# Encoder block: softmax scaling ahead of the fillers, gates by tanh, half of branch B's maxima on VectorE, first remainders on VectorE

## Chip, core and metric

The kernel runs on one core of a Trainium2 chip. The metric is the device time of one execution in microseconds (us). TensorE is called PE below, VectorE DVE, ScalarE ACT, GpSimd POOL and SyncE, which issues the DMAs, SP.

## The reference

One encoder layer on 512 tokens of 1024 channels, in float32. Attention is a mixer of two branches, and the gates decide how much of each goes on.

```python
h    = layer_norm(x, ln0_g, ln0_b)
proj = h @ w_in                                    # 1024 -> 5120: q, k, v of both branches, gate columns ga, gb
ya   = gqa_blocked(qa, ka, va) @ w_branch_a        # branch A: 8 query heads, 2 key heads, dense softmax
ob   = sum over 3 groups of weight_g * dilated_band_attention_g   # branch B: 12 heads in 3 groups
yb   = ob @ w_branch_b
gates  = sigmoid(concat(ga, gb) + b_gate)
merged = gates[:, :1024] * ya + gates[:, 1024:] * yb
h = layer_norm(alpha * h + merged @ w_out)
h = layer_norm(alpha * h + expert_choice_ffn(h))   # router, top-k of 64 tokens, 16 experts of SwiGLU
```

Each group of branch B masks its scores (`s = where(mask, s * scale, -1e30)`), and its weight in the sum is the softmax over the groups of the log of its softmax denominator.

## The kernel before, in words

Every matrix product of the attention part is done in three matmuls on a split operand: `hi` is the value cast to the rounded type `fp32r`, `lo` is the remainder `value - hi`, and `mm3` (lines 242 to 244) adds hi*hi, lo*hi and hi*lo into one PSUM bank. Weights come in tiles of 128 x 1024. `split(i)` makes `whl[i % 4]` of tile i: the cast on ACT (L216), the remainder on DVE (L221); for tiles 1 to 3 the remainder is on POOL (also L221), and for tile 0 half is on DVE (L218) and half on POOL (L219).

The order of the instructions is written out by hand, and every engine works through its own list in that order. The input projection has ten chunks c = 0 to 9 of 512 columns; a chunk is 32 units (8 slices k, 4 row blocks m), and a unit is one `mm3`. All units but those of chunk 0 are put into a queue, and `fill(ns)` takes units from it, 650 to a unit, together with the casts, remainders, PSUM copies and rotary steps that hang on them. These are the fillers: they stand on all engines between the steps of the attention. Chunks 6 to 9 are the gates, 0 to 5 everything else; the products with `w_branch_a` and `w_branch_b` (`branch_units`) are queued as well.

At the start, `ln0_norm(i)` (L301) normalises 128 rows, `h_transpose` (L319) transposes them on PE, and `h_split` applies gain and bias (L330 on ACT, L332 on DVE) and splits the result (L335, L338). The rsqrt of the norm ends in three small DVE steps (L136 to L138). `keep_clock` (L609) is matmuls whose result nobody reads.

Branch A has 16 items of 128 queries by two heads. An item transposes the probabilities of the item before (`a_trans`, L748), multiplies those of two items before with v (`a_pv`, L759), makes its scores, and `a_soft` takes the maximum (L732, L734, DVE) and the exponential with its sum (L736, ACT). Then come `fill(3 * UNIT)`, `a_norm`, which takes the reciprocal (L740) and scales both heads' probabilities (L743) on DVE, and `fill(3 * UNIT)`.

Branch B has 8 items, each with two heads s = 0 and 1. `b_trans` (L844), `b_pv` (L857) and `b_scores` (L811, L815) are on PE. `b_soft` does for each s: scale and mask (L833, DVE), the maximum per block (L835), its negative (L836), and one exponential per block with the negative maximum as bias and the sum as a by-product (L838, ACT; 2 blocks of 256 in group 0, 4 of 128 in the others). `fill(7 * UNIT)` ends an item. Then the groups are weighed together in two halves (`combine1`, `combine2`; L926 is the last kind of matmul in it, L929 to L934 its last vector steps).

`evac_gate(c)` adds the gate's bias on DVE from PSUM (L679, per m) and applies one sigmoid to all four m (L681, 128 x 2048, ACT); for c = 9 there is one sigmoid per m from PSUM (L677). PSUM has four banks for these units (`ps_pj`), and a bank is free again when its evacuation has read it.

After the output projection and the router come the 16 experts. Their weights come in loads of 2 MB, issued by SP (L1026) into a ring of eight slots; a slot is loaded again when what used its memory before is done. Gate and up projections are L1414, down projections L1451.

Of the kernel before, what the change touches and what calls it, by code (L numbers as in the profile page):

```python
# [17 lines left out]
P = 128  # L18
S = 512
D = 1024  # L20
NT = S // P
# [26 lines left out]
def encoder_block(ctx, tc, x, ln0_g, ln0_b, w_in, b_gate, qn_g, kn_g, w_branch_a, w_branch_b,  # L48
# [158 lines left out]

    wo = [None, None]

    def split(i):  # L210

        load_to(i + 1)
        hi = whl[i % 4][:, 0].rearrange("p k c -> p (k c)")
        lo = whl[i % 4][:, 1].rearrange("p k c -> p (k c)")
        r = stage(i)
        A.copy(hi, r)  # L216
        if i == 0:
            V.tensor_tensor(lo[:, 0:512], r[:, 0:512], hi[:, 0:512].bitcast(F32), OP.subtract)  # L218
            G.tensor_tensor(lo[:, 512:1024], r[:, 512:1024], hi[:, 512:1024].bitcast(F32), OP.subtract)  # L219
        else:  # L220
            (G if i < 4 else V).tensor_tensor(lo, r, hi.bitcast(F32), OP.subtract)  # L221
        load_to(min(NSTREAM, max(6, i + 3) if i < 3 else i + 5 if i < 7 else max(12, i + 3)))

    done_split = [0]
# [95 lines left out]
            pts.append(pt)  # L320
        return pts

    def h_split(i, pts, then=None):

        t = xin[i].rearrange("p (k t) -> p k t", k=KT)

        def gain(k):
            src, g_, b_ = pts[k // 4][:, (k % 4) * P:(k % 4 + 1) * P], gcol[:, k:k + 1], gcol[:, KT + k:KT + k + 1]
            if k >= 4:
                A.activation(t[:, k, :], src, AF.Identity, bias=b_, scale=g_)  # L330
            else:
                V.tensor_scalar(t[:, k, :], src, g_, b_, op0=OP.mult, op1=OP.add)  # L332

        def hi(q):
            A.copy(hT[0][:, 4 * q:4 * q + 4, i * P:(i + 1) * P], t[:, 4 * q:4 * q + 4, :])  # L335

        def lo(q):
            V.tensor_tensor(hT[1][:, 4 * q:4 * q + 4, i * P:(i + 1) * P], t[:, 4 * q:4 * q + 4, :],  # L338
                            hT[0][:, 4 * q:4 * q + 4, i * P:(i + 1) * P].bitcast(F32), OP.subtract)

        for k in range(4):
            gain(k)
        gain(4)
        gain(5)
        if then is not None:
            ln0_stats(then, 0)
        hi(0)
        lo(0)
        gain(6)
        gain(7)  # L350
        if then is not None:
            ln0_stats(then, 1)
        hi(1)
        lo(1)
# [262 lines left out]
    keep_clock(4)  # L617
    A.copy(gcol, pt[:, 0:2 * KT])
    ln0_norm(0, mvy)
    split_to(2)  # L620
    pts = h_transpose(0)
    keep_clock(4)
    h_split(0, pts, 1)
    split_to(3)
    mvy = ln0_var(1)
    split_to(4)
    ln0_norm(1, mvy)
    for m in range(NT):
        gemm0(m, 0, 4)
        if m + 1 < NT:  # L630
# [32 lines left out]
    def gate_bias():  # L663
        pt = bank("t")
        T.transpose(pt[:, 0:16], gb[0:16, 0:P], ident[0:16, 0:16])
        V.tensor_copy(bg, pt[:, 0:16])

    gemm_units(5, True, evac5, after(chain_b, lambda m: t_b(2, m)) + [(24, gate_bias)])

    def evac_gate(c):  # L670
        b = 4 * ((c - 6) % 2)

        def ev(m):
            gt = merged[:, b:b + 4] if c < 8 else gsig
            o = 4 * (c - 6) + m
            if c == 9:
                A.activation(gt[:, m, :], pj[c, m], AF.Sigmoid, bias=bg[:, o:o + 1])  # L677
                return
            V.tensor_scalar(gt[:, m, :], pj[c, m], bg[:, o:o + 1], None, op0=OP.add)  # L679
            if m == NT - 1:  # L680
                A.activation(gt, gt, AF.Sigmoid)  # L681
        return ev

    def branch_units(c):
        nk = 4 if c < 8 else 2
        for m in range(NT):
# [13 lines left out]
            def ev(m=m):  # L700
                mg = merged[:, 4 * ((c - 6) % 2) + m]
                if c < 8:
                    V.tensor_tensor(mg, pj[c, m, 1], mg, OP.mult)
                else:
                    V.tensor_tensor(gsig[:, m, :], pj[c, m, 1], gsig[:, m, :], OP.mult)
                    V.tensor_tensor(mg, mg, gsig[:, m, :], OP.add)
            queue.append((0.0, ev))

# [5 lines left out]


    fill_until("chain1")

    def a_scores(p, i):
        kv = p // 2
# [48 lines left out]
    for n in range(len(items) + 1):  # L768
# [13 lines left out]
            ln0_gain(n)  # L782
        if n == 8:
            dma(gb[0:16, 0:P], b_gate.rearrange("o (j p) -> (o j) p", p=P))
        fill(3 * UNIT)
        if n < len(items):
            a_norm(sm, n % 2)
            fill(3 * UNIT)
    a_pv(*items[-1], (len(items) - 1) % 2)
    gates.add("A")  # L790
    cp[1] = 2
# [28 lines left out]
    def b_soft(g, p, ii, st, n):  # L820
        nb = 2 if g == 0 else 4
        i0 = 2 * ii
        for s in range(2):
# [9 lines left out]
            V.scalar_tensor_tensor(pv, sv, SCALE, mask, op0=OP.mult, op1=OP.add)  # L833
            mg, dg = stat_of(0, g, h), stat_of(1, g, h)
            V.tensor_reduce(mg[:, i0:i0 + nb], pv, axis=AX.X, op=OP.max)  # L835
            V.tensor_scalar(ng[:, 0:nb], mg[:, i0:i0 + nb], -1.0, None, op0=OP.mult)  # L836
            for b in range(nb):
                A.activation(pv[:, b, :], pv[:, b, :], AF.Exp, bias=ng[:, b:b + 1], accum_out=dg[:, i0 + b:i0 + b + 1])  # L838

    def b_trans(n, s):  # L840
        pt = bank("t")
# [25 lines left out]
    for n in range(len(items) + 2):  # L867
# [8 lines left out]
            b_pv(g, p, ii, n - 2, g > 0 or ii == 1)  # L876
        if n < len(items):
            st = b_scores(*items[n])
            b_soft(*items[n], st, n)
        fill((7 if n < len(items) else 1) * UNIT)  # L880
    side[0] = None


# [68 lines left out]
    def merged_split(q, eng=V):  # L952

        t = mhl4[order[q]]
        mg = merged[:, 2 * q:2 * q + 2]
        A.copy(t[:, :, 0], mg)
        eng.tensor_tensor(t[:, :, 1], mg, t[:, :, 0].bitcast(F32), OP.subtract)

    def block_hi(k):
        A.copy(mhl4[order[k // 2]][:, k % 2, 0], merged[:, k])  # L960

    def block_lo(k):
        t = mhl4[order[k // 2]][:, k % 2]
        V.tensor_tensor(t[:, 1], merged[:, k], t[:, 0].bitcast(F32), OP.subtract)

    branch_units(8)
    gemm_units(9, False, evac_gate(9), [(18, lambda: merged_split(0)), (26, lambda: merged_split(1))])
# [714 lines left out]
```

## Time and profile before

| | us |
|---|---|
| median of 3 runs | 1393.04 |
| lowest and highest | 1390.86, 1393.53 |
| the profiled execution, its own time | 1393.52 |
| its span in the profile | 1391.5 |
| PE busy | 1287.9 (93%) |
| DVE busy | 443.5 (32%) |
| ACT busy | 282.9 (20%) |
| POOL busy | 24.9 (2%) |

The span is the time from the first to the last recorded instruction; the execution's own time is 2.02 us longer. The attention part, with the output projection, lies before about 390 us of the span; the experts fill the rest up to the last norm. A share over the whole span mixes the two, so the stretches are read apart below. The granted PE clock is given as a part of full speed: 1.00 is 2.4 GHz and 0.50 is 1.2 GHz.

### The profile page before, as it was taken

What the parts mean: (1) busy time and instruction counts of PE and PEld (TensorE: products, weight loads), DVE (VectorE), ACT (ScalarE), POOL (GpSimd) and SP (SyncE); (2) the same over time, 40 slices, a digit from 0 to 9 for tenths busy, and PEclk for the clock granted to TensorE, in tenths of its full rate; (3) what the DMA queues carried; (4) which work ended last, traced back from release to release, by engine and by line L of the source; (5) the groups of instructions that cost most, each with busy time, mean ns of one, the idle gap of its engine ahead of it and who ended that gap; (6) DMA issues with size and microseconds to landing.
All of it is one profiled execution on the core that took longest, in us unless ns stands there. A gap on an engine that the chain in (4) does not pass through costs nothing.

```text
span 1391.5 us, 15293 instructions
## 1 busy us (share of the span) xinstructions
PE 1287.9 (93%) x6404; PEld 659.1 (47%) x6404; DVE 443.5 (32%) x836; ACT 282.9 (20%) x592; POOL 24.9 (2%) x20
## 2 busy tenths in 40 slices
PE   7999999999999999999999789979979988997994
PEld 5888888777887334333333223323323332332342
DVE  7876554666475122020030011102002101210206
ACT  4555444634224010010000001000000000010101
POOL 2000000000020000000000000000000000000001
PEclk9999999999999999999999999999999999999998
DMA  7122111115278789999999999999999999999994
GB/s 265 55 76 61 47 46 46 61 46 182 80 289 338 312 365 428 428 426 427 429 428 426 428 429 426 426 428 429 427 428 428 426 429 427 428 427 428 427 375 172
DMA packets 61323, 440.05 MB, mean 316 GB/s; under 512 B 7659, under 2 KB 23323, under 8 KB 36935
## 3 DMA queue, kind: packets, MB, share of 16 engines
q1 hardware_dynamic: 61255, 439.08, 76.9%
q8 instruction: 50, 0.82, 0.2%
q14 instruction: 18, 0.15, 0.0%
HBM read 436.96 MB, written 2.10 MB: 316 GB/s over the span
## 4 chain that ended last, share of the span: by engine, by line
PE 63%; DMA 25%; DVE 7%; ACT 3%; issue 1%; ACTq 0%; DVEq 0%
DMA ring<-in_w_up_e_dram 18%; PE ps_pj L1414 15%; PE ps_o L1451 14%; DMA ring<-in_w_down_e_dram 7%; PE ps_pj L242 6%; PE ps_pj L243 5%; PE ps_pj L244 5%; PE ps_x L1464 4%; PE ps_x L1362 3%; PE ps_o L759 1%; PE ps_x L748 1%; PE ps_pj L1516 1%; DVE whl L221 1%; PE ps_x L1378 1%; ACT whl L216 1%
## 5 line engine op out<-in xcount | busy, mean ns | idle before, releaser
L1414 PE MATMUL ps_pj<-ring,misc 128*64 128x512 f32 x2032 | 449.6, 595 | 53.6 <-DMA ring<-in_w_up_e_dram 28.5
L1414 PEld LDWEIGHTS ps_pj<-ring,misc 128*64 128x64 f32 x2032 | 144.7, 137 | 349.4 <-issue 295.0
L1451 PE MATMUL ps_o<-ring,misc 128*64 128x512 f32 x928 | 219.2, 602 | 6.3 <-DVE misc L454 2.1
L1427 DVE SCALAR_TENSOR_TENSOR misc<-misc,gate,ps_pj 128x512 f32<-128x512 f32 x32 | 23.8, 747 | 444.0 <-PE ps_pj L1414 365.5
L1451 PEld LDWEIGHTS ps_o<-ring,misc 128*64 128x64 f32 x928 | 58.8, 136 | 138.9 <-issue 126.0
L1426 ACT ACTIVATE misc<-ps_pj 128x512 f32<-128x512 f32 x32 | 19.0, 597 | 365.2 <-PE ps_pj L1414 365.2
L242 PE MATMUL ps_pj<-whl,hT 128*128 128x512 f32 x192 | 78.3, 408 | 0.5 <-ACT hT L335 0.5
L243 PE MATMUL ps_pj<-whl,hT 128*128 128x512 f32 x192 | 76.4, 398 | 1.5 <-DVE hT L338 1.5
L244 PE MATMUL ps_pj<-whl,hT 128*128 128x512 f32 x192 | 76.3, 398 | 0.0
L1466 DVE TENSOR_TENSOR merged<-merged,ps_x 128x512 f32<-128x512 f32 x56 | 38.4, 686 | 103.2 <-PE ps_x L1464 103.2
L1383 ACT ACTIVATE misc<-ps_x,ln_bcol,ln_gcol 128x64 f32<-128x64 f32 x64 | 25.8, 403 | 212.0 <-DVE misc L1385 212.0
L1464 PE MATMUL ps_x<-misc,cst 128*128 128x512 f32 x112 | 63.0, 645 | 0.0
L221 DVE TENSOR_TENSOR whl<-misc,whl 128x1024 fp32r<-128x1024 f32 x38 | 46.1, 1222 | 36.7 <-ACT whl L216 36.7
L1362 PE MATMUL ps_x<-hbuf,misc 128*64 128x512 f32 x256 | 57.7, 593 | 0.0
L1385 DVE TENSOR_SCALAR misc<-ps_x,ln_gcol,ln_bcol 128x64 f32<-128x64 f32 x64 | 22.0, 344 | 106.3 <-PE ps_x L1378 83.6
L242 PE MATMUL ps_pj<-hT,whl 128*128 128x512 f32 x128 | 51.9, 406 | 0.9 <-ACT misc L452 0.7
L243 PEld LDWEIGHTS ps_pj<-whl,hT 128*128 128x128 f32 x192 | 48.3, 252 | 5.7 <-DVE hT L338 2.2
L242 PEld LDWEIGHTS ps_pj<-whl,hT 128*128 128x128 f32 x192 | 48.2, 251 | 5.5 <-ACT hT L335 0.9
L244 PE MATMUL ps_pj<-hT,whl 128*128 128x512 f32 x128 | 49.9, 390 | 0.0
L244 PEld LDWEIGHTS ps_pj<-whl,hT 128*128 128x128 f32 x192 | 48.1, 250 | 3.9
L243 PE MATMUL ps_pj<-hT,whl 128*128 128x512 f32 x128 | 49.9, 390 | 0.0
L216 ACT CAST whl<-misc 128x1024 fp32r<-128x1024 f32 x38 | 39.4, 1044 | 21.7 <-DMA misc<-in_w_branch_b_dram 8.5
(322 smaller groups left out, 1280.8 us busy)
## 6 DMA issues: line engine op xcount, KB each, us to landing
ring<-in_w_gate_e_dram SPq DMA_DIRECT2D x63, 2048.0 KB, 30.1
ring<-in_w_up_e_dram SPq DMA_DIRECT2D x62, 2048.0 KB, 26.2
ring<-in_w_down_e_dram SPq DMA_DIRECT2D x57, 2048.0 KB, 31.8
misc<-in_w_in_dram SPq DMA_DIRECT2D x22, 512.0 KB, 3.7
ring<-in_w_down_e_dram SPq DMA_DIRECT2D x12, 512.0 KB, 8.1
misc<-in_w_in_dram SPq DMA_DIRECT2D x20, 256.0 KB, 3.1
misc<-in_w_out_dram SPq DMA_DIRECT2D x8, 512.0 KB, 4.5
b_qk<-in_w_in_dram SPq DMA_DIRECT2D x6, 512.0 KB, 6.8
```

What stands on the lines that cost most here:

```text
L216: A.copy(hi, r)
L221: (G if i < 4 else V).tensor_tensor(lo, r, hi.bitcast(F32), OP.subtract)
L242: T.matmul(out_, sh, mh, start=start, stop=False)
L243: T.matmul(out_, sl, mh, start=False, stop=False)
L244: T.matmul(out_, sh, ml, start=False, stop=stop)
L1362: T.matmul(pg[64 * g:64 * g + 64, :], oneh[:, m, s * CAP:(s + 1) * CAP], zk[:, :, 4 * g:4 * g + 4], start=m == 0, stop=m == NT - 1)
L1383: A.activation(xeT[e % 2][:, k, :], src, AF.Identity, bias=bcol[:, k:k + 1], scale=gcol[:, k:k + 1])
L1414: T.matmul(gu[which][t // 2][(t % 2) * 64:(t % 2) * 64 + 64, :], xe[:, k, :], w[:, kk % 2, :, 4 * t:4 * t + 4], start=k == 0, stop=k == KT ...
L1427: V.scalar_tensor_tensor(hh[t], sg[t], gate[e], gu[1][t], op0=OP.mult, op1=OP.mult)
L1451: T.matmul(py[n * 64:n * 64 + 64, :], hTe[:, j, :], w[:, n * 512:(n + 1) * 512], start=i == 0, stop=i == 15)
L1464: T.matmul(po, scat[:, m, :], ye[:, n * 512:(n + 1) * 512], start=True, stop=True)
L1466: V.tensor_tensor(a, a, po, OP.add)
```

## The change

- Remainders of tiles 1 to 3 (L221 on POOL) are on DVE: that of tile 1 inside `h_split(0)`, those of tiles 2 and 3 behind `ln0_norm(1)`. Half of tile 0 stays on POOL.
- `a_norm` stands ahead of all six units of an item.
- The gates are `tanh(0.5 x + 0.5 b)`, on ACT straight from PSUM, per m; the multiply is `(t + 1) * product`, and the factor 0.5 that is left is applied where `merged` is split. The table set of exp is loaded ahead of branch A by a line of its own.
- In branch B, s = 0 is as before. For s = 1 DVE subtracts the maximum (one 128 x 512 instruction), ACT does one exponential of 128 x 512, and DVE sums per block (`b_sum`). An item has `fill(3 * UNIT)`, `b_sum`, `fill(3 * UNIT)` where it had `fill(7 * UNIT)`.

```diff
@@ -207,18 +207,22 @@
     wo = [None, None]
-    def split(i):
+    def split(i, then=True):
         load_to(i + 1)
+        A.copy(whl[i % 4][:, 0].rearrange("p k c -> p (k c)"), stage(i))
+        if then:
+            split_lo(i)
+
+    def split_lo(i):
         hi = whl[i % 4][:, 0].rearrange("p k c -> p (k c)")
         lo = whl[i % 4][:, 1].rearrange("p k c -> p (k c)")
         r = stage(i)
-        A.copy(hi, r)
         if i == 0:
             V.tensor_tensor(lo[:, 0:512], r[:, 0:512], hi[:, 0:512].bitcast(F32), OP.subtract)
             G.tensor_tensor(lo[:, 512:1024], r[:, 512:1024], hi[:, 512:1024].bitcast(F32), OP.subtract)
         else:
-            (G if i < 4 else V).tensor_tensor(lo, r, hi.bitcast(F32), OP.subtract)
+            V.tensor_tensor(lo, r, hi.bitcast(F32), OP.subtract)
         load_to(min(NSTREAM, max(6, i + 3) if i < 3 else i + 5 if i < 7 else max(12, i + 3)))
     done_split = [0]
@@ -320,7 +324,7 @@
             pts.append(pt)
         return pts
-    def h_split(i, pts, then=None):
+    def h_split(i, pts, then=None, mid=None):
         t = xin[i].rearrange("p (k t) -> p k t", k=KT)
@@ -346,6 +350,8 @@
             ln0_stats(then, 0)
         hi(0)
         lo(0)
+        if mid is not None:
+            mid()
         gain(6)
         gain(7)
         if then is not None:
@@ -617,14 +623,18 @@
     keep_clock(4)
     A.copy(gcol, pt[:, 0:2 * KT])
     ln0_norm(0, mvy)
-    split_to(2)
+    split(0)
+    split(1, False)
     pts = h_transpose(0)
     keep_clock(4)
-    h_split(0, pts, 1)
-    split_to(3)
+    h_split(0, pts, 1, lambda: split_lo(1))
+    split(2, False)
     mvy = ln0_var(1)
-    split_to(4)
+    split(3, False)
     ln0_norm(1, mvy)
+    split_lo(2)
+    split_lo(3)
+    done_split[0] = 4
     for m in range(NT):
         gemm0(m, 0, 4)
         if m + 1 < NT:
@@ -663,22 +673,18 @@
     def gate_bias():
         pt = bank("t")
         T.transpose(pt[:, 0:16], gb[0:16, 0:P], ident[0:16, 0:16])
-        V.tensor_copy(bg, pt[:, 0:16])
+        V.tensor_scalar(bg, pt[:, 0:16], 0.5, None, op0=OP.mult)
     gemm_units(5, True, evac5, after(chain_b, lambda m: t_b(2, m)) + [(24, gate_bias)])
     def evac_gate(c):
+
         b = 4 * ((c - 6) % 2)
         def ev(m):
             gt = merged[:, b:b + 4] if c < 8 else gsig
             o = 4 * (c - 6) + m
-            if c == 9:
-                A.activation(gt[:, m, :], pj[c, m], AF.Sigmoid, bias=bg[:, o:o + 1])
-                return
-            V.tensor_scalar(gt[:, m, :], pj[c, m], bg[:, o:o + 1], None, op0=OP.add)
-            if m == NT - 1:
-                A.activation(gt, gt, AF.Sigmoid)
+            A.activation(gt[:, m, :], pj[c, m], AF.Tanh, bias=bg[:, o:o + 1], scale=0.5)
         return ev
     def branch_units(c):
@@ -700,9 +706,9 @@
             def ev(m=m):
                 mg = merged[:, 4 * ((c - 6) % 2) + m]
                 if c < 8:
-                    V.tensor_tensor(mg, pj[c, m, 1], mg, OP.mult)
+                    V.scalar_tensor_tensor(mg, mg, 1.0, pj[c, m, 1], op0=OP.add, op1=OP.mult)
                 else:
-                    V.tensor_tensor(gsig[:, m, :], pj[c, m, 1], gsig[:, m, :], OP.mult)
+                    V.scalar_tensor_tensor(gsig[:, m, :], gsig[:, m, :], 1.0, pj[c, m, 1], op0=OP.add, op1=OP.mult)
                     V.tensor_tensor(mg, mg, gsig[:, m, :], OP.add)
             queue.append((0.0, ev))
@@ -714,6 +720,7 @@
     fill_until("chain1")
+    A.preload_act_table_set("exp_and_others")
     def a_scores(p, i):
         kv = p // 2
@@ -782,10 +789,9 @@
             ln0_gain(n)
         if n == 8:
             dma(gb[0:16, 0:P], b_gate.rearrange("o (j p) -> (o j) p", p=P))
-        fill(3 * UNIT)
         if n < len(items):
             a_norm(sm, n % 2)
-            fill(3 * UNIT)
+        fill((6 if n < len(items) else 3) * UNIT)
     a_pv(*items[-1], (len(items) - 1) % 2)
     gates.add("A")
     cp[1] = 2
@@ -833,9 +839,14 @@
             V.scalar_tensor_tensor(pv, sv, SCALE, mask, op0=OP.mult, op1=OP.add)
             mg, dg = stat_of(0, g, h), stat_of(1, g, h)
             V.tensor_reduce(mg[:, i0:i0 + nb], pv, axis=AX.X, op=OP.max)
-            V.tensor_scalar(ng[:, 0:nb], mg[:, i0:i0 + nb], -1.0, None, op0=OP.mult)
-            for b in range(nb):
-                A.activation(pv[:, b, :], pv[:, b, :], AF.Exp, bias=ng[:, b:b + 1], accum_out=dg[:, i0 + b:i0 + b + 1])
+            if s == 0:
+                V.tensor_scalar(ng[:, 0:nb], mg[:, i0:i0 + nb], -1.0, None, op0=OP.mult)
+                for b in range(nb):
+                    A.activation(pv[:, b, :], pv[:, b, :], AF.Exp, bias=ng[:, b:b + 1], accum_out=dg[:, i0 + b:i0 + b + 1])
+            else:
+                V.tensor_tensor(pv, pv, mg[:, i0:i0 + nb].unsqueeze(2).to_broadcast([P, nb, 512 // nb]), OP.subtract)
+                A.activation(pr, pr, AF.Exp)
+        return lambda: V.tensor_reduce(dg[:, i0:i0 + nb], pv, axis=AX.X, op=OP.add)
     def b_trans(n, s):
         pt = bank("t")
@@ -876,8 +887,10 @@
             b_pv(g, p, ii, n - 2, g > 0 or ii == 1)
         if n < len(items):
             st = b_scores(*items[n])
-            b_soft(*items[n], st, n)
-        fill((7 if n < len(items) else 1) * UNIT)
+            b_sum = b_soft(*items[n], st, n)
+            fill(3 * UNIT)
+            b_sum()
+        fill((3 if n < len(items) else 1) * UNIT)
     side[0] = None
@@ -953,15 +966,15 @@
         t = mhl4[order[q]]
         mg = merged[:, 2 * q:2 * q + 2]
-        A.copy(t[:, :, 0], mg)
-        eng.tensor_tensor(t[:, :, 1], mg, t[:, :, 0].bitcast(F32), OP.subtract)
+        A.activation(t[:, :, 0], mg, AF.Copy, scale=0.5)
+        eng.scalar_tensor_tensor(t[:, :, 1], mg, 0.5, t[:, :, 0].bitcast(F32), op0=OP.mult, op1=OP.subtract)
     def block_hi(k):
-        A.copy(mhl4[order[k // 2]][:, k % 2, 0], merged[:, k])
+        A.activation(mhl4[order[k // 2]][:, k % 2, 0], merged[:, k], AF.Copy, scale=0.5)
     def block_lo(k):
         t = mhl4[order[k // 2]][:, k % 2]
-        V.tensor_tensor(t[:, 1], merged[:, k], t[:, 0].bitcast(F32), OP.subtract)
+        V.scalar_tensor_tensor(t[:, 1], merged[:, k], 0.5, t[:, 0].bitcast(F32), op0=OP.mult, op1=OP.subtract)
     branch_units(8)
     gemm_units(9, False, evac_gate(9), [(18, lambda: merged_split(0)), (26, lambda: merged_split(1))])
```

Three places show what that does to the engines' lists. The lines of the changed kernel are 4 to 13 higher for the same code. First DVE at the start; `hT_68` is the remainder of the transposed rows (L338, in the changed kernel L342), `whl_69` and `whl_70` are weight tiles. Before:

```order
L338 TENSOR_TENSOR hT_68<-merged,hT_67 128x4x128
L148 BN_STATS ln_st<-merged 128x6
L338 TENSOR_TENSOR hT_68<-merged,hT_67 128x4x128
L291 BN_AGGR ln_mv<-ln_st 128x2
L292 TENSOR_SCALAR ln_mv<-ln_mv 128x1
L136 TENSOR_TENSOR newton<-ln_y 128x1
L137 SCALAR_TENSOR_TENSOR newton<-newton,ln_mv 128x1
L138 SCALAR_TENSOR_TENSOR ln_mv<-newton,ln_y 128x1
L301 TENSOR_SCALAR hbuf<-merged,ln_mv 128x1024
L148 BN_STATS ln_st<-merged 128x6 x2
```

And of the change:

```order
L342 TENSOR_TENSOR hT_68<-merged,hT_67 128x4x128
L225 TENSOR_TENSOR whl_69<-b_qk,whl_69 128x1024
L148 BN_STATS ln_st<-merged 128x6
L342 TENSOR_TENSOR hT_68<-merged,hT_67 128x4x128
L295 BN_AGGR ln_mv<-ln_st 128x2
L296 TENSOR_SCALAR ln_mv<-ln_mv 128x1
L136 TENSOR_TENSOR newton<-ln_y 128x1
L137 SCALAR_TENSOR_TENSOR newton<-newton,ln_mv 128x1
L138 SCALAR_TENSOR_TENSOR ln_mv<-newton,ln_y 128x1
L305 TENSOR_SCALAR hbuf<-merged,ln_mv 128x1024
L225 TENSOR_TENSOR whl_70<-b_qk,whl_70 128x1024 x2
L148 BN_STATS ln_st<-merged 128x6 x2
```

The remainder of tile 1 comes in behind the first `hT` remainder, and two more (tiles 2 and 3) behind the norm of the second 128 rows, ahead of the statistics of the third. On POOL one instruction is left here, L219 (L223 in the changed kernel).

Second DVE in an item of branch A that has a weight tile and rotary steps (L517 to L521; L523 to L527 in the changed kernel) among its fillers. Before:

```order
L732 TENSOR_REDUCE asm<-ps_x 128x1
L734 TENSOR_SCALAR asm<-asm,qsc 128x1
L221 TENSOR_TENSOR whl_70<-misc,whl_70 128x1024
L517 TENSOR_TENSOR misc<-misc,cst 128x512
L519 TENSOR_TENSOR misc<-misc,cst 128x32x8 x2
L521 TENSOR_TENSOR misc<-misc 128x32x16
L740 RECIPROCAL asm<-asm 128x2
L743 TENSOR_SCALAR merged<-merged,asm 128x512 x2
L454 COPY merged<-ps_x 128x512
```

And of the change:

```order
L739 TENSOR_REDUCE asm<-ps_x 128x1
L741 TENSOR_SCALAR asm<-asm,qsc 128x1
L747 RECIPROCAL asm<-asm 128x2
L750 TENSOR_SCALAR merged<-merged,asm 128x512 x2
L225 TENSOR_TENSOR whl_70<-misc,whl_70 128x1024
L523 TENSOR_TENSOR misc<-misc,cst 128x512
L525 TENSOR_TENSOR misc<-misc,cst 128x32x8 x2
L527 TENSOR_TENSOR misc<-misc 128x32x16
L460 COPY merged<-ps_x 128x512
```

The reciprocal and the two scalings (L740, L743; L747, L750) stand right behind the maxima, and the weight remainder and the rotary steps follow them.

Third ACT in branch B, at the first gate chunk. Before, from the exponentials of item 4 to those of item 5:

```order
L838 ACTIVATE misc,cst<-misc,bng 128x128 x8
L681 ACT_TABLE_LOAD
L681 ACTIVATE merged<-merged 128x2048
L216 CAST whl_70<-misc 128x1024 x2
L452 COPY misc<-ps_x 128x512
L452 COPY b_qk<-ps_o 128x512
L838 ACT_TABLE_LOAD
L838 ACTIVATE misc,cst<-misc,bng 128x128 x8
```

And of the change, from the exponentials of item 4 (L845, L848) to those of item 5 and what follows them:

```order
L845 ACTIVATE misc,cst<-misc,bng 128x128 x4
L848 ACTIVATE misc<-misc 128x512
L213 CAST whl_69<-misc 128x1024
L687 ACTIVATE merged<-ps_pj,misc 128x512 x2
L458 COPY misc<-ps_x 128x512
L458 COPY b_qk<-ps_o 128x512
L845 ACTIVATE misc,cst<-misc,bng 128x128 x4
L848 ACTIVATE misc<-misc 128x512
L687 ACTIVATE merged<-ps_pj,misc 128x512 x2
L213 CAST whl_70<-misc 128x1024 x2
```

Both table loads are gone, eight exponentials in an item are five, and the gate's evacuation is four tanh (L687) in two pairs in two items, where it was a single sigmoid behind four additions on DVE. The order of PE's matmuls shifts because an item of branch B takes six units: seven units of the projection stood between the last L926 and the first unit of the product with `w_branch_a` before, and fifteen stand there (behind L939, its new line) in the changed kernel. The numbers of matmuls are the same.

## Rows read from the trace of the kernel before

**Rows 1.** Stretches: length, busy (instructions) per engine, clock, DMA share, GB/s.
```profile
90.00:200.00 110.00, 102.69 (x622) 93.34 (x622) 69.53 (x142) 55.40 (x111) 0.00 (x0) 0.97 0.18 53
...
225.00:300.00 75.00, 72.29 (x462) 58.34 (x459) 46.62 (x77) 40.58 (x122) 0.20 (x1) 0.95 0.16 50
...
520.00:1340.00 820.00, 760.82 (x3516) 257.70 (x3514) 116.58 (x203) 64.74 (x144) 0.00 (x0) 1.00 1.01 427
```

**Rows 2.** Waits of SP's queue: waiter, releaser, us, times, longest.
```profile
SPq L1026 <- PE ps_pj L244: 34.6, 3, 12.3
```

**Rows 3.** Waits of PE from 90 to 200 us, same columns.
```profile
PE ps_x L748 <- DVE merged L743: 6.7, 4, 3.5
```

**Rows 4.** Waits of PE from 225 to 330 us, same columns.
```profile
PE ps_pj L242 <- DVE merged L679: 2.4, 1, 2.4
PE ps_x L815 <- ACT misc L452: 2.0, 1, 2.0
```

**Rows 5.** Short stretches, PE alone: length, busy (instructions), clock, DMA share, GB/s.
```profile
183.60:190.30 6.70, 5.34 (x28) 0.50 0.21 72
...
269.00:275.60 6.60, 6.59 (x19) 0.50 0.48 159
...
323.50:326.90 3.40, 3.40 (x10) 0.51 0.93 319
```

**Rows 6.** Timeline in branch A: start, length, engine, line, tiles [idle before, releaser].
```profile
178.66 0.78 ACT L736 ACTIVATE merged<-ps_x,asm,qsc 128x512 f32<-128x512 f32 x1
...
180.99 1.22 DVE L221 TENSOR_TENSOR whl<-misc,whl 128x1024 fp32r<-128x1024 f32 x1 [2.36 <-ACT whl L216]
...
184.33 0.88 DVE L743 TENSOR_SCALAR merged<-merged,asm 128x512 f32<-128x512 f32 x2
...
184.96 1.94 PE L748 MATMUL ps_x<-cst,merged 128*128 128x128 f32 x8 [3.47 <-DVE merged L743]
```

**Rows 7.** Timeline at the start of branch A, ACT.
```profile
91.50 0.78 ACT L736 ACTIVATE merged<-ps_x,asm,qsc 128x512 f32<-128x512 f32 x1 [1.91 <-DVE asm L734]
```

**Rows 8.** Timeline in branch B, item 4 and what follows it.
```profile
258.46 0.69 DVE L833 SCALAR_TENSOR_TENSOR misc<-ps_x,cst 128x512 f32<-128x512 f32 x1 [0.56 <-PE ps_x L815]
...
263.39 1.28 ACT L681 ACT_TABLE_LOAD   x1
...
264.69 1.91 ACT L681 ACTIVATE merged<-merged 128x2048 f32<-128x2048 f32 x1
...
269.01 2.07 PE L815 MATMUL ps_x<-b_qk 64*128 64x128 f32 x8 [2.04 <-ACT misc L452]
```

**Rows 9.** Timeline behind combine2.
```profile
321.87 2.72 DVE L679 TENSOR_SCALAR merged<-ps_pj,misc 128x512 f32<-128x512 f32 x4
...
327.80 0.39 PE L242 MATMUL ps_pj<-a_qk,whl 128*128 128x512 f32 x1
...
328.48 0.39 PE L242 MATMUL ps_pj<-a_qk,whl 128*128 128x512 f32 x1
```

**Rows 10.** Timeline of the start.
```profile
10.69 1.79 DVE L338 TENSOR_TENSOR hT<-merged,hT 128x512 fp32r<-128x512 f32 x1 [0.20 <-ACT hT L335]
...
13.04 5.21 POOL L221 TENSOR_TENSOR whl<-b_qk,whl 128x1024 fp32r<-128x1024 f32 x2 [1.11 <-ACT whl L216]
...
14.48 1.44 DVE L136 TENSOR_TENSOR newton<-ln_y 128x1 f32<-128x1 f32 x1 [0.50 <-ACT ln_y L295]
...
15.96 2.31 DVE L137 SCALAR_TENSOR_TENSOR newton<-newton,ln_mv 128x1 f32<-128x1 f32 x1
...
18.30 0.16 DVE L138 SCALAR_TENSOR_TENSOR ln_mv<-newton,ln_y 128x1 f32<-128x1 f32 x1
...
19.37 1.10 PE L319 MATMUL ps_x<-cst,hbuf 128*128 128x128 f32 x8 [1.54 <-DVE hbuf L301]
...
22.91 0.69 DVE L338 TENSOR_TENSOR hT<-merged,hT 128x512 fp32r<-128x512 f32 x1
...
23.65 0.51 PE L243 MATMUL ps_pj<-whl,hT 128*128 128x512 f32 x1 [0.21 <-DVE hT L338]
```

## The prediction, made before the changed kernel ran

> **What bounds the kernel now.** I read the table of stretches first, then the waits of SP and PE, then the clock of short stretches, then the timeline where a wait ends. In the experts' stretch the DMA share is 1.01 while PE idles 59 of 820 us [rows 1]: the weight stream sets the pace there, and nothing in this change touches it. But the stream cannot begin early: its first loads wait for PE's projection units, 34.6 us in three waits [rows 2]. A microsecond taken out ahead of them lets all loads start that much earlier, so I pass on what the attention part gains in full.
>
> In the attention part PE is the engine that matters. It idles 7.3 of 110 us in branch A (110 - 102.69) and 2.7 of 75 us in branch B [rows 1]. In A, 6.7 us of that is one kind of wait: the transposes L748 wait for the scalings L743 on DVE, four times, longest 3.5 [rows 3]. In B and behind it there are two waits of note: 2.0 us for a copy on ACT, and 2.4 us for the bias additions L679 [rows 4].
>
> The waits have a second price. Right after the waits of 3.47 and 2.04 us in the timeline, and after the one of 2.4 us, the granted clock is 0.50, 1.2 GHz, for 6.7, 6.6 and 3.4 us [rows 5, 6, 8]. At half the clock half of PE's busy time there is lost: 5.34 / 2 = 2.7, 6.59 / 2 = 3.3 and 3.40 / 2 = 1.7 us.
>
> **Branch A.** The longest wait reads like this: the second exponential ends at 178.66 + 0.78 = 179.44, but DVE's list has a weight remainder (at 180.99) and the rotary steps ahead of the scaling, which starts at 184.33; PE has been idle since 184.96 - 3.47 = 181.49 [rows 6]. The change puts reciprocal and scaling right behind the maxima. They follow the exponential by the scaling's 0.88, a reciprocal ahead of it (0.16, as the small step L138 [rows 10]) and handovers: done at about 180.7, 0.8 us before PE needs it. The rotary steps then come about 1.1 us later. They feed chunks some units on, and PE shows no wait for them in A, so I cost that at nothing; if that cover is gone, 1.1 us in the few items that have such steps, 3 us in all. Gain: 6.7 us of wait and 2.7 us of clock, 9.4. Bounds: 6 (three waits shrink, the clock term stays) and 9.4.
>
> The new table load at A's start takes 1.28 us, as the one in B does [rows 8]; ACT idles 1.91 us ahead of the first exponential [rows 7], so it is hidden. In these rows the next activation starts 0.02 us after the load's end (263.39 + 1.28 = 264.67, then 264.69). The Trainium skill, "ScalarE: Activation LUTs", section "What ACT_TABLE_LOAD costs", adds a drain of 1.38 us and gives 2.66 us for each switch; that would exceed the idle time by 0.75 us and make the sum 0.75 smaller in gain. The trace has no such drain, so the sum goes by 1.28.
>
> **Branch B.** Per item one STT and one maximum for each s stay. For s = 1 the negation (a small step, 0.16) and four exponentials go (two of 256 in group 0); a subtraction, one exponential of 512 and a sum come. None of the three stands in the trace of before; the nearest rows are the STT of 128 x 512 on DVE (0.69 [rows 8]) and A's exponential of 128 x 512 (0.78 [rows 6]). Bounds for each: 0.44 (one of the two scalings in 0.88) and 1.22 (a remainder of 1024 columns) [rows 6]. I take the 0.69 and 0.78, which have the shape. From the start of the first STT the exponentials of s = 1 are ready after five DVE steps of 0.69, a small one of 0.16 and 0.78 on ACT: 4.4 us. Before, they were ready by 263.39 - 258.46 = 4.9 us [rows 8]. So ACT's chain is shorter by 0.5 us, but the cover shrinks as well: a unit is 0.68 us (328.48 - 327.80 [rows 9]), six are 4.1 instead of 4.8, with some 0.5 us of scores left ahead of them. Margin before 0.4, now 0.2 us.
>
> Behind the exponentials the sum adds 0.69 on DVE, with a weight remainder (1.22 [rows 6]) ahead of it in most items, and the copy of the transposes for the next step stands behind both. That copy can come late: 4.4 + 1.1 of a cast on ACT + 1.2 + 0.7 = 7.4 us after the STT, where the transposes end at 4.6 + 1.0. PE has about 1.1 us of `b_pv` and three banks in hand. I put this at 0.4 us in each of eight items, 3.2 us; bounds 0 and, with the subtraction or the exponential at its upper bound, 0.9 each, 7 in all.
>
> What goes: the wait of 2.04 us behind the sigmoid. It came from ACT being taken 1.28 us by a table load, 1.91 by the sigmoid of 128 x 2048 and two casts ahead of the copy [rows 8]; now four tanh (0.78 each by the exponential's row, which reads PSUM as well) stand in two pairs in two items, and no load. With it go the rest of B's idle time, 2.7 us in all [rows 1], and 3.3 us of half clock [rows 5]. Sum for B: -6.0 + 3.2 = -2.8, bounds -6 and +1. The eight units that leave B cost the same later, since PE's matmuls are the same.
>
> **Behind combine2.** PE waits 2.4 us for a bank that the additions L679 free [rows 4]; these start at 321.87, when DVE comes out of the combine [rows 9]. In the changed program fifteen instead of seven units stand there, 8 x 0.68 = 5.4 us more of work for PE to do while DVE finishes the combine, and the banks are freed by tanh on ACT. A casting of a weight tile (about 1 us) stands between two of the tanh; that is well inside 5.4. Gain 2.4 + 1.7 of clock = 4.1; bounds 2 and 4.1. The multiplication by STT, and the split with a factor, have the operands and the size of what they replace (0.69 and 1.22 for the same shapes); I take 0, at most 0.1 us each on a part that PE does not wait for.
>
> **The start.** While POOL works on its remainders (13.04, 5.21 us for two), DVE's instructions are long: L338 takes 1.79 at 10.69 and 0.69 at 22.91, and the steps L136 and L137 take 1.44 and 2.31 where L138 right behind takes 0.16 [rows 10]. Without POOL I take 1.1, 1.3 and 2.1 us off, and add 1.2 for the remainder of tile 1: the transposes L319 start at 19.37 - 3.3 = 16.1. Then two remainders stand ahead of the next statistics, 2 x 1.22 = 2.4, so the first matmul that needs the second block's remainder (23.65) comes 3.3 - 2.4 = 0.9 us earlier. But PE runs out of work: after transposes of 0.9 and four units of 2.7 us it is idle from about 19.7 to 22.2, and every wait of 2 us or more in the rows above was followed by half clock. I price that as the one of 3.4 us, 1.7. The start is then 0.8 us longer. Bounds: -0.9 (no half clock) and +2.4 (a stretch as in B, 3.3). SP's loads wait on these remainders too; POOL's second ended at 18.25, DVE's will at about 18.5, so the loads keep their time.
>
> **Sum.** +0.8 - 9.4 - 2.8 - 4.1 = -15.5 us. The profiled execution took 1393.52 us, 2.02 more than its span, and lies 0.48 above the median of the runs: 1393.52 - 15.5 = 1378.0. Against the median this is 1.1% less.
>
> **The rivals.**
> - *More of it:* B's item period falls to PE's work, no new waits (-6.0), and the start loses nothing (-0.9). For it: DVE is busy 46.6 and ACT 40.6 of 75 us in B [rows 1]. Against it: margins of 0.2 us. -0.9 - 9.4 - 6.0 - 4.1 = -20.4: 1373.
> - *Less of it:* the wait in B is replaced by another of 2 us with its half clock (B 0), and the start has the long dip (+2.4). -9.4 - 4.1 + 2.4 = -11.1: 1382.5. For it: the copies queue behind cast, remainder and sum.
> - *No change:* the stream of experts has slack of its own and swallows the gain, 1393. Against it: SP's waits at its beginning are for PE [rows 2].
> - *Slower:* in B the copies come over 2 us late, because remainder, sum and copy stand in one line on DVE; in four of them, those with a weight remainder, that is 8 us, and each wait brings a stretch of half clock like the one of 3.3 us, 13 us. Nothing is gained in B then: 8 + 13 + 2.4 at the start - 9.4 - 4.1 = +9.9, 1403. It decides where the copy comes 2 us after PE could have gone on. For it: the estimate of 7.4 us; against it: the two heads' copies go to both engines, and in the items of before, with 4.9 us and the same remainder behind, no such wait shows but the one [rows 4].
>
> **How the numbers follow.** The forecast has 0.50, more 0.20, less 0.18, no change 0.06, slower 0.06. The forecast's own range is 1374 to 1383, since the bounds of four terms (together -20.4 and -4.6) hardly fall to one side at once. To leave out no more than 2 in 10 I take 1370 to 1386. Less than 0.2% (2.8 us) cannot be told from no change here. All of the first three are below 1390: 0.88 with the chances of that; 0.06 the same; 0.06 slower.
>
> **What would show it.** In the profile after: no wait of L748's counterpart for the scaling on DVE, and clock 1.00 from 90 to 200 us; three table loads up to the output projection instead of five; the gap behind combine2 gone; in B no single wait over 1 us and clock 1.00; a PE idle of about 2.5 us near 20 us, perhaps with half clock; first expert loads some 15 us earlier and the experts' part as long as before. It would be wrong if B shows waits for DVE copies in most items, if half clock appears in a new place, or if the experts' part grows by what the attention part lost.

## The result, and the profile after

The changed kernel takes 1374.62 us (median of 4 runs, 1373.76 to 1375.31); the kernel before, run beside it, 1393.28 us (4 runs, 1390.86 to 1394.63). The ratio is 0.9872 with a 95% interval of 0.986 to 0.9885: 18.7 us less. The forecast was 1378.0 with a range of 1370 to 1386. The profiled execution took 1375.31 us, its span is 1373.5.

These are the three stretches of [rows 1] after the change, with the same columns:

```profile
90.00:200.00 110.00, 109.40 (x682) 100.72 (x681) 74.96 (x156) 62.01 (x124) 0.00 (x0) 1.00 0.20 58
...
225.00:300.00 75.00, 73.44 (x467) 56.31 (x466) 56.00 (x89) 31.66 (x78) 0.20 (x1) 1.00 0.18 55
...
520.00:1340.00 820.00, 761.11 (x3534) 260.18 (x3532) 115.84 (x203) 67.23 (x147) 0.00 (x0) 1.00 1.01 425
```

PE's idle time in branch A falls from 7.3 to 0.6 us, and the clock there is 1.00. In B the clock is 1.00 too, but 1.6 us of idle time stay, and DVE is busy for 56.0 instead of 46.6 us. The experts' stretch is as before, DMA share 1.01. (The first stretch begins at the same place in the program before and after the change, within half a microsecond; the second begins some 10 us and the third some 18 us further on.)

The waits of PE from 90 to 200 us, and then from 225 to 330 us (waiter, releaser, us in total, times, longest); they answer to [rows 3, 4]:

```profile
PE ps_x L731 <- ACT merged L458: 0.4, 1, 0.4
PE ps_x L755 <- ACT whl L213: 0.2, 1, 0.2
```

```profile
PE ps_x L855 <- ACT misc L848: 1.4, 4, 0.7
```

No wait for the scaling on DVE, none for a copy in B (one of 0.2 us stands before 225), none behind combine2; one new kind, the transposes of B (L855) for the exponential of s = 1 (L848). Up to the output projection ACT loads three tables instead of five.

The item of A that waited longest [rows 6], after the change (start, length, engine, line, tiles, idle before and its releaser):

```profile
176.12 0.17 DVE L747 RECIPROCAL asm<-asm 128x2 f32<-128x2 f32 x1 [0.94 <-ACT merged L743]
176.33 0.89 DVE L750 TENSOR_SCALAR merged<-merged,asm 128x512 f32<-128x512 f32 x2
177.56 1.22 DVE L225 TENSOR_TENSOR whl<-misc,whl 128x1024 fp32r<-128x1024 f32 x1 [0.34 <-ACT whl L213]
178.70 0.69 DVE L523 TENSOR_TENSOR misc<-misc,cst 128x512 f32<-128x512 f32 x1
```

The scaling starts at 176.33, ahead of the weight remainder and the rotary steps. And ACT at A's start [rows 7]:

```profile
89.65 0.37 ACT L458 COPY b_qk<-ps_x 128x256 f32<-128x256 f32 x1
90.04 1.28 ACT L723 ACT_TABLE_LOAD   x1
91.93 0.78 ACT L743 ACTIVATE merged<-ps_x,asm,qsc 128x512 f32<-128x512 f32 x1 [0.61 <-DVE asm L741]
```

The new table load lies in ACT's idle time; 0.61 us are left after its end at 91.32.

The start [rows 10]:

```profile
14.79 0.16 DVE L137 SCALAR_TENSOR_TENSOR newton<-newton,ln_mv 128x1 f32<-128x1 f32 x1
...
15.91 2.35 DVE L225 TENSOR_TENSOR whl<-b_qk,whl 128x1024 fp32r<-128x1024 f32 x2
...
16.05 1.10 PE L323 MATMUL ps_x<-cst,hbuf 128*128 128x128 f32 x8 [0.82 <-DVE hbuf L305]
...
21.88 0.50 PE L246 MATMUL ps_pj<-whl,hT 128*128 128x512 f32 x1 [1.98 <-ACT hT L339]
...
22.61 0.49 PE L247 MATMUL ps_pj<-whl,hT 128*128 128x512 f32 x1 [0.23 <-DVE hT L342]
```

The small DVE steps take 0.16 us with POOL idle, the transposes start at 16.05 instead of 19.37, and the first matmul with the second block's remainder at 22.61 instead of 23.65. PE is idle for 1.98 us ahead of 21.88.

To see where the time came from I compare the start of one and the same matmul of the program in both traces. After the start (matmul 80) the changed kernel is 0.45 us late, 0.36 of which is there from the first matmul on, which waits for a DMA. At the end of A (matmul 1140) it is 9.67 us early. In B the time from the first item's first STT (`SCALAR_TENSOR_TENSOR`, the scale and mask of `b_soft`) to the last item's takes 56.33 instead of 64.06 us, and seven units of 0.68 have left it: 3.0 us of gain. Well behind combine2 (matmul 1760) it is 16.96 us early, so 7.3 - 3.0 = 4.3 us came behind combine2. By matmul 1920 it is 17.47 us early: another 0.5 us, which the sum of the prediction does not have. The first expert load, before and after:

```profile
390.38 0.80 SPq L1026 DMA_DIRECT2D ring<-in_w_gate_e_dram  x2
```

```profile
372.91 0.80 SPq L1039 DMA_DIRECT2D ring<-in_w_gate_e_dram  x2
```

It is issued 17.5 us earlier, and the span is 18.0 us shorter: the experts' part passes the gain on.

### The profile page after: what moved, and what is told of

It reads as the page before. It is cut to its first block, busy times and chain, and to the rows that moved or that the text cites. A ratio compares the mean times of both kernels' runs of the same rounds, so it can differ in the third digit from the quotient of the medians.

```text
span 1373.5 us, 15252 instructions
## 1 busy us (share of the span) xinstructions
PE 1280.5 (93%) x6404; PEld 653.7 (48%) x6404; DVE 443.1 (32%) x835; ACT 277.0 (20%) x559; POOL 17.2 (1%) x17
## 4 chain that ended last, share of the span: by engine, by line
PE 64%; DMA 26%; DVE 7%; ACT 2%; issue 1%; SPq 0%; ACTq 0%; DVEq 0%
DMA ring<-in_w_up_e_dram 18%; PE ps_pj L1427 15%; PE ps_o L1464 14%; DMA ring<-in_w_down_e_dram 7%; PE ps_pj L246 6%; PE ps_pj L247 6%; PE ps_pj L248 6%; PE ps_x L1477 4%; PE ps_x L1375 3%; PE ps_o L766 1%; PE ps_x L755 1%; DVE whl L225 1%; PE ps_pj L1529 1%; PE ps_x L731 1%; PE ps_x L1391 1%
```

## The experiments

Each kernel ran in five rounds beside the kernel before. In that company the kernel before spread over 1387 to 1395 us, so ratios have intervals of 0.3 to 0.6%. Smaller differences are read from the traces, one profile for each kernel.

**The norm put back between the fillers.**

```diff
-        if n < len(items):
-            a_norm(sm, n % 2)
-        fill((6 if n < len(items) else 3) * UNIT)
+        fill(3 * UNIT)
+        if n < len(items):
+            a_norm(sm, n % 2)
+            fill(3 * UNIT)
```

> The changed kernel with a_norm put back between two blocks of three fillers. Theory (each wait for the scaling on DVE, with the half clock behind the longest one, is what A gained): the waits of L755 return with about 6.7 us and one stretch of half clock, A is 9 to 10 us longer, 1384 us. Rival (A gained because the table load and the gates' work were moved, the place of the scaling only shifts the wait to another line): 1375 to 1377 us.

Measured: 1385.48 us, ratio to before 0.9957 (0.9942 to 0.9972), 10.9 us over the median of the changed kernel; in the profiles the spans differ by 9.0. The longest entry of PE's waits from 90 to 225 us, and its clock behind the last of them:

```profile
PE ps_x L755 <- DVE merged L750: 6.7, 4, 3.5
```

```profile
185.50:188.90 3.40, 3.40 (x20) 0.50 0.00 0
```

It is the row of before to the digit, four waits, 6.7 us, with tanh and everything else in place. From matmul 80 to 1120 A is 9.1 us longer: 6.7 of waits and 2.4 more. The half clock lasts 3.4 us here, so it explains 3.40 / 2 = 1.7 of the 2.4; in the kernel before it lasted 6.7 us behind the same wait of 3.5 [rows 5]. The rival falls.

**The remainders back on POOL.**

```diff
-            V.tensor_tensor(lo, r, hi.bitcast(F32), OP.subtract)
+            (G if i < 4 else V).tensor_tensor(lo, r, hi.bitcast(F32), OP.subtract)
```

The calls of `split` at the start stand as before, too.

> The changed kernel with the remainders of tiles 1 to 3 on POOL and in their old place. Theory (the start gained 1.0 us at its last late matmul and lost about as much to a new PE idle and its half clock): within 1 us of the changed kernel, 1374 to 1375.5 us, the idle of 2 us near 20 us gone, half clock near 13 us back. Rival (DVE being slow while POOL works is worth more than that): 1377 us or more.

Measured: 1373.94 us, ratio 0.9877 (0.9857 to 0.9897): no difference to the changed kernel that can be told. The start's waits of PE, then its clock near 13 and 20 us (length, busy, clock, DMA share, GB/s), and two of DVE's small steps:

```profile
PE ps_x L323 <- DVE hbuf L305: 3.1, 1, 3.1
PE ps_pj L247 <- DVE hT L342: 1.5, 2, 1.3
```

```profile
12.90:16.30 3.40, 3.31 (x15) 1.00 1.04 392
20.30:24.00 3.70, 3.52 (x16) 1.00 0.23 56
```

```profile
14.42 1.48 DVE L136 TENSOR_TENSOR newton<-ln_y 128x1 f32<-128x1 f32 x1 [0.50 <-ACT ln_y L299]
15.93 2.27 DVE L137 SCALAR_TENSOR_TENSOR newton<-newton,ln_mv 128x1 f32<-128x1 f32 x1
```

In the kernel before the same wait for `hT`, and the clock behind it, were:

```profile
PE ps_pj L243 <- DVE hT L338: 1.5, 2, 1.3
```

```profile
12.90:16.30 3.40, 3.40 (x10) 0.51 1.03 392
```

The waits for DVE come back as expected, 1.3 us ahead of 12.9 and 3.1 for the norm, and so do the long steps on DVE. But the half clock expected near 13 us does not: the clock stays at 1.00 after both waits, where the same 1.3 us were followed by 0.51 in the kernel before. The wait of 3.1 us is the first row against the prediction's reading that waits of 2 us or more are followed by half clock.

**Seven units in branch B.**

```diff
-        fill((3 if n < len(items) else 1) * UNIT)
+        fill((4 if n < len(items) else 1) * UNIT)
```

> The changed kernel with seven units per item of branch B (three, the sum, four). Theory (the wait behind combine2 went because eight more units stand there): the waits of B (1.4 us) go, the wait behind combine2 and its half clock come back in part, 1375 to 1378 us. Rival (that wait went because tanh on ACT frees the bank): no wait behind combine2, 1373 us.

Measured: 1375.28 us, ratio 0.9881 (0.9861 to 0.9902). PE's waits from 215 to 335 us:

```profile
PE ps_pj L246 <- ACT merged L687: 1.6, 1, 1.6
PE ps_pj L246 <- ACT misc L458: 0.7, 1, 0.7
```

The waits for the exponential are gone, a copy is waited for again as in the kernel before (0.7 us), and 1.6 us stand behind combine2, now for the tanh. The net is 0.5 us in favour of seven units in the trace (from 0.81 later than the changed kernel at matmul 80 to 0.30 later at 1920). So the units behind combine2 did matter, as the theory has it, but with tanh only 1.6 of the 2.4 us come back, and the half clock does not.

**The gates by sigmoid again.**

```diff
-            A.activation(gt[:, m, :], pj[c, m], AF.Tanh, bias=bg[:, o:o + 1], scale=0.5)
+            if c == 9:
+                A.activation(gt[:, m, :], pj[c, m], AF.Sigmoid, bias=bg[:, o:o + 1])
+                return
+            V.tensor_scalar(gt[:, m, :], pj[c, m], bg[:, o:o + 1], None, op0=OP.add)
+            if m == NT - 1:
+                A.activation(gt, gt, AF.Sigmoid)
```

With it the factors of 0.5, the multiply by (t + 1) and the early table load are out.

> The changed kernel with the gates as before: bias added on DVE, one sigmoid of 128 x 2048, no factor 0.5. Theory (table loads and the long sigmoid on ACT held up B's copies): a wait of about 2 us for a copy on ACT with half clock behind it in B, up to 5 us, 1377 to 1380 us, nothing behind combine2 because fifteen units stand there. Rival (fewer exponentials and the order of the units did it alone): 1374.6 us, no wait over 1 us in B.

Measured: 1381.69 us, ratio 0.9931 (0.9914 to 0.9947), 7.1 us over the changed kernel, a little more than expected. The timeline of ACT and PE at the first gate chunk, then PE's waits, then its clock:

```profile
258.77 1.28 ACT L691 ACT_TABLE_LOAD   x1
...
260.07 1.91 ACT L691 ACTIVATE merged<-merged 128x2048 f32<-128x2048 f32 x1
...
261.88 1.97 ACT L213 CAST whl<-misc 128x1024 fp32r<-128x1024 f32 x2
...
263.76 0.57 ACT L458 COPY misc<-ps_x 128x512 f32<-128x512 f32 x1
...
264.39 2.07 PE L824 MATMUL ps_x<-b_qk 64*128 64x128 f32 x8 [2.82 <-ACT misc L458]
```

```profile
PE ps_x L824 <- ACT misc L458: 2.8, 1, 2.8
PE ps_x L858 <- ACT misc L851: 0.8, 3, 0.3
PE ps_pj L246 <- DVE merged L689: 0.6, 1, 0.6
```

```profile
267.00:270.40 3.40, 3.40 (x10) 0.50 0.64 185
```

It is the picture of [rows 8]: load, sigmoid, two casts, and only then the copy that PE waits for, 2.8 us now, with half clock from 267 to 270.4. Behind combine2 0.6 us of the 2.4 are back, where none was expected. Between matmuls 80 and 1920 the program is 6.4 us longer: 4.6 in B (matmuls 1140 to 1700), 1.1 from there to 1760, and 0.6 behind it, where the changed kernel had gained 0.5 beyond the sum. The tanh is what freed B. A stays as it is without the early table load (181.8 us from matmul 80 to 1140, 181.7 with it).

**Branch B's softmax as before, gates by tanh.**

```diff
-            if s == 0:
-                V.tensor_scalar(ng[:, 0:nb], mg[:, i0:i0 + nb], -1.0, None, op0=OP.mult)
-                for b in range(nb):
-                    A.activation(pv[:, b, :], pv[:, b, :], AF.Exp, bias=ng[:, b:b + 1], accum_out=dg[:, i0 + b:i0 + b + 1])
-            else:
-                ...
+            V.tensor_scalar(ng[:, 0:nb], mg[:, i0:i0 + nb], -1.0, None, op0=OP.mult)
+            for b in range(nb):
+                A.activation(pv[:, b, :], pv[:, b, :], AF.Exp, bias=ng[:, b:b + 1], accum_out=dg[:, i0 + b:i0 + b + 1])
```

Seven units follow in one block, without `b_sum`.

> The changed kernel with branch B's softmax as before (one exponential per block for both heads, seven units per item); gates stay tanh. Theory (in B the tanh is what gained, the half of the maxima on DVE gains nothing by itself): no wait over 1 us in B, a wait of 1.5 to 2.4 us behind combine2, within 2 us of the changed kernel, 1373 to 1377. Rival (ACT's shorter chain is needed): waits for ACT in several items of B, 1378 us or more.

Measured: 1375.26 us, ratio 0.9885 (0.9857 to 0.9913). PE's waits from 215 to 340 us:

```profile
PE ps_pj L246 <- ACT merged L687: 1.6, 1, 1.6
PE ps_pj L246 <- ACT misc L458: 0.7, 1, 0.7
```

The theory holds: nothing over 1 us in B, 1.6 us behind combine2. From matmul 1140 to 1760 it takes 107.58 us, the changed kernel 107.26, the kernel before 114.56. Moving half of the maxima to DVE and the fillers with it is worth 0.3 us: B itself is 1.6 us shorter without it (59.48 us from the first to the last item's first STT, against 56.33 and seven units of 0.68), and the stretch behind it 1.9 longer.

**PE kept busy at the start.**

```diff
     for m in range(NT):
+        if m == 1:
+            keep_clock(8)
         gemm0(m, 0, 4)
```

> The changed kernel with eight matmuls whose result nobody reads in PE's idle of 2.0 us near 20 us. Theory (that idle is what brings half clock at 23 us in some executions): clock 1.00 from 20 to 30 us, the first matmul of the second block at the same time, 0 to 1.7 us less than the changed kernel, 1373 to 1374.6. Rival (the clock falls for another reason, by chance): half clock there or elsewhere at the start, no difference.

Measured: 1373.83 us, ratio 0.9876 (0.9852 to 0.99). **Later statistics**, with the statistics of the third block handed to `h_split` and those of the fourth behind the third norm:

```diff
-                ln0_stats(2, 0)
-                ln0_stats(2, 1)
-                mvy = ln0_var(2)
 ...
+                def stats2():
+                    ln0_stats(2, 0)
+                    ln0_stats(2, 1)
+                h_split(1, pts, None, stats2)
+ ...
```

> The changed kernel with the statistics of the third 128 rows moved behind the first remainder of the second block, and those of the fourth behind the third norm. Theory (DVE's list sets the start: statistics stand ahead of the gains): the first matmul of the second block about 1.6 us earlier, a wait for the third norm of up to 1.5 us instead, start 1 to 3 us shorter: 1371.5 to 1373.5. Rival (the third norm comes late and PE waits as long there): 1374 to 1376.

Measured: 1374.05 us, ratio 0.9875 (0.9852 to 0.9899). PE's clock from 23.25 to 26.6 us in the changed kernel, with PE kept busy, and in two runs whose start is the changed kernel's, the norm put back and B undone:

```profile
23.25:26.60 3.35, 3.35 (x10) 0.52 0.33 82
```

```profile
23.25:26.60 3.35, 3.35 (x20) 1.00 0.32 77
```

```profile
23.25:26.60 3.35, 3.35 (x20) 1.00 0.34 85
```

```profile
23.25:26.60 3.35, 3.35 (x20) 1.00 0.34 86
```

With the idle time filled the clock is full, as the theory has it. But it is full as well in the last two, with the same wait of 2.0 us. Five profiles have this start (after, the norm put back, seven units, sigmoid, B undone); half clock follows in two, after and seven units. So one profile cannot prove that the filling helped, and the runs do not: 1373.72 to 1375.58, where the changed kernel has 1373.76 to 1375.31. Moving the statistics trades the wait of 2.0 us for 1.2 at the third norm. From the first matmul to number 160 it takes 40.5 us; the changed kernel's profile, with half clock, takes 41.4, but the three profiles of its start with full clock 40.3 to 40.4. So nothing is saved where the clock holds, and the 1 to 3 us that were expected are not there: the time is the rival's.

**Both together:** the later statistics, and `fill((4 if n in (1, 2, 6) else 3 if n < len(items) else 1) * UNIT)` in B.

> The start of the run with later statistics, and seven units instead of six in three items of branch B, so that eleven or twelve units stand behind combine2. Theory (waits of B go with the seventh unit, and those units are not needed behind combine2): waits of L855 for the exponential gone in these items, no wait behind combine2, 0.5 to 1 us less than the run with later statistics. Rival (each seventh unit only moves a wait): the same time.

Measured: 1373.92 us, ratio 0.9874 (0.9851 to 0.9897), not apart from the changed kernel or from the later statistics alone (1374.05). PE's waits from 215 to 340 us:

```profile
PE ps_x L862 <- ACT misc L855: 0.7, 1, 0.7
PE ps_o L879 <- DVE b_qk L460: 0.5, 1, 0.5
```

Of the 1.4 us of waits for the exponential 0.7 are left in one item, and 0.5 for a copy has come. From matmul 160 to 1920 it is 0.7 us shorter than the later statistics alone, so the waits did go, as the theory has it. But of the 2.0 us that its program is ahead of the changed kernel's at matmul 1920 its span keeps 1.2, and the span of the later statistics alone is no longer (1372.1 against 1372.3). The time is the rival's; where the 0.8 us went behind matmul 1920 is not shown.

## Why the prediction was right, point by point

- **Branch A, -9.4 forecast, -10.1 measured.** Right in place and size. The waits are the 6.7 us of [rows 3]; the norm put back restores them alone. The rest is 3.4 us here and 2.4 with the norm put back. Half clock explains 2.7 of the first, as forecast, and 1.7 of the second, where it lasted half as long; the 0.7 us left in both are not in the forecast, and what they are is not shown.
- **Start, +0.8 forecast, about +0.1 measured** (0.45 less the 0.36 of the first DMA). This is the term that was mis-sized. The late matmul came 1.04 us earlier in the trace and 1.4 counted from the first matmul (0.9 forecast), and half clock followed in that profile, worth 1.5 us: between matmuls 40 and 80 the two profiles with half clock take 12.4 us, the three without 10.9. But the step "every wait of 2 us or more in the rows above was followed by half clock" is wrong as a rule: five profiles with the same wait of 2.0 us show it twice, and with the remainders on POOL a wait of 3.1 us was followed by none. Counted from the first matmul the start is 0.9 to 1.0 us shorter than before in the three, the forecast's lower bound, and the same within 0.1 in the two. Which of the two the profile of the result would show, the prediction could not tell.
- **Branch B, -2.8 forecast, -3.0 measured.** Right in its terms, wrong in one place. PE in B (length, busy, clock, DMA share, GB/s), before and after:

```profile
225.72:289.78 64.06, 61.35 (x384) 0.95 0.16 51
```

```profile
216.05:272.38 56.33, 54.58 (x363) 1.00 0.19 57
```

The transposes alone in the same stretches (L844, L855), and in B's old softmax with tanh (L850), where nothing waits for the exponential of s = 1:

```profile
225.72:289.78 64.06, 7.24 (x56) 0.95 0.16 51
```

```profile
216.05:272.38 56.33, 8.55 (x56) 1.00 0.19 57
```

```profile
214.90:274.38 59.48, 7.25 (x56) 1.00 0.18 55
```

The 2.71 us of idle time of before went, and 1.75 of new idle time came. The new waits cost more than that: the transposes that wait are also booked as busy for 8.55 us instead of 7.24, so together they cost 1.75 + 1.31 = 3.1, where the forecast had 3.2. PE's busy time fell by 6.77 us; 4.76 of that are the seven units, and with the 1.31 added back the lost half clock is 3.3, as forecast. But the new waits are at another place than the copy: the transposes wait for the exponential. The queue is the one forecast (remainder, sum, copy on DVE); that it delays the next STT, and through it the exponential, fits these rows but was not tested by itself.
- **What in B did it.** The forecast put the gain on the sigmoid and its table loads, and the runs agree: the sigmoid put back costs B 4.6 us, and B's old softmax with tanh makes B 1.6 shorter; 4.6 - 1.6 are the 3.0 measured. The shorter chain on ACT bought B nothing, because the cover shrank by a unit; what it gave stands behind combine2.
- **Behind combine2, -4.1 forecast, -4.3 measured.** Two causes, and either alone ends the half clock: with seven units and tanh 1.6 us of wait stay, with fifteen units and the sigmoid 0.6. The forecast named both without dividing them.
- **What the sum did not have.** The span fell by 18.0 us, 2.4 more than the sum of -15.5. The start (with its DMA), A, B and combine2 account for some 1.4 of it. The rest lies behind combine2's stretch: 0.5 us between matmuls 1760 and 1920, gone again with the sigmoid and so from the gates' change, and 0.5 behind the first expert load. So the measured time lies nearer to the rival "more of it" (1373) than to the forecast (1378). Half of that rival came true, a start that loses nothing; its other half, B without new waits, did not.
- **Passing through.** The rival "no change" fell: the loads began 17.5 us earlier and the span ends 18.0 earlier. This holds within 1 us only: over the nine profiles of changed kernels the span's gain on before and the lead at matmul 2000 differ by -0.4 to +0.9. "Less of it" and "slower" fell with B, where no single wait is over 0.7 us. The other 0.7 us between 18.0 and the medians' 18.7 is within the spread of the kernel before.
- **The table load.** The row at 90.04 shows 1.28 us and then 0.61 of idle time, with no wait of PE behind it beyond the 0.4 us that stood there before. The drain of 1.38 us that the Trainium skill adds ("ScalarE: Activation LUTs", section "What ACT_TABLE_LOAD costs") does not show: it would have put the exponential at 92.70, and it starts at 91.93; ahead of the load ACT has 0.02 us free.

What stays open is why the clock falls after one wait of 2.0 us and not after the next. The kernel before has three waits of over 2 us and spreads over 1387 to 1395 us in the rounds; the changed kernel has one of 2.0 and spreads over 1.5 us. The clock on record goes with that spread: of the twelve runs of the kernel before beside the first four experiments, the two fastest (1387.14 and 1387.73) had a mean granted clock of 0.993 and 0.992, the two slowest (1394.94 and 1394.09) 0.987 and 0.988. That the three waits decide it is argued, not shown.

## What to carry to other kernels

Where engines work through lists in a fixed order, a short step on another engine that the next matmul needs belongs ahead of the fillers, which can come any time: that alone was 9 to 10 us here. A function with its own table set costs most where a copy for PE queues behind load, function and casts, so look at what stands behind it and not at its own 1.28 us. A cover of fillers and a chain that shrink together give nothing there: here 0.3 us in all. And a wait can cost more than the idle time that is booked for it, where the instructions that wait are booked as longer: compare their busy time with a run in which they do not wait.

## What was not expected of the hardware

- The same start with the same PE wait of 2.0 us ran on at a granted clock of 1.00 in three profiles and at 0.52 to 0.57 in two (23.25 to 26.6 us). Behind the same wait of 3.5 us in A half clock lasted 6.7 us in one kernel and 3.4 in another.
- DVE's one-column steps took 1.44 and 2.31 us while POOL worked on its remainders, 0.16 each once POOL's work was on DVE, and 1.48 and 2.27 when it was given back to POOL. Still, giving it back changed the time by less than can be told (1373.94 against 1374.62). In the traces the first 160 matmuls take 40.7 us with it, between the 40.3 to 40.4 and the 41.1 to 41.4 of the start on DVE with full and with half clock: two remainders on DVE (2.35 us) stand ahead of the next statistics there.
